# Forming the low halves of split weights by an accumulating DMA instead of a VectorE subtraction

## The chip, the core and the metric

The kernel runs on one core of one Trainium2 chip. The metric is the device time of one execution in microseconds (us): the median of several runs, and beside it one execution taken by the hardware profiler, from which every row below comes. The engines are called as in the profile: PE is TensorE's matmul side and PEld its weight loads, DVE is VectorE, ACT is ScalarE, POOL is GpSimd, and SP is the engine that here only issues transfers. Sixteen DMA engines move the data between memory and the core.

## The reference, cut to what matters

Two decoder layers work on 272 tokens (16 meta tokens and 256 of the input) of width 1024. All matrix products are taken in float32:

```
for l in range(2):
    h = rms_norm(x, norm1_g[l])
    u = h @ w_in[l]                       # 1024 x 6560, split among three mixers and their gates
    y_a = conv_module(...); y_b = mla(...); y_c = hgrn2(...)
    mix = gate_a * y_a + gate_b * y_b + gate_c * y_c
    x = x + mix @ w_out[l]                # 1024 x 1024
    h2 = rms_norm(x, norm2_g[l])
    x = x + square(relu(h2 @ w_ff1[l])) @ w_ff2[l]   # 1024 x 4096 x 1024
return x[:, 16:]
```

The weights are read once: 146 MB in all, most of it w_in, w_ff1 and w_ff2.

## The kernel before, in words

A float32 product is made of three matmuls in the reduced type float32r. Every weight and every activation is split into a high part, which is the value rounded to float32r, and a low part, which is the value minus its high part. The helper `mm3` then adds high by high, low by high and high by low (lines 208, 209 and 210).

The weights come in pieces of 128 partitions by 1024 columns of float32, 512 KB each. There are 276 such pieces, and each serves 24 matmuls. `piece` (line 193) brings one: `fetch` (line 104) has SP load it into a buffer `wraw`, of which there are three; ACT rounds it into `whi` (line 198), of which there are four; DVE subtracts `whi` from `wraw` into `wlo` (line 200), of which there are four as well. A `wraw` buffer is free for the next load when ACT and DVE have both read it. A `whi` or `wlo` buffer is free when PE has used the last of its columns.

Each layer has two parts. In the mixer part (66 pieces: w_in, the two latent projections and the branches' output projections) the tiles of `h @ w_in` alternate with the steps of the attention, the HGRN2 recurrence and the convolution, whose small operations lie on DVE, ACT, POOL and PE; the order is set by rates in the code. In the feed-forward part (72 pieces: w_out, w_ff1, w_ff2) there is little besides the pieces and their matmuls.

The order on each engine comes from the framework's scheduler. `piece` raises its priority by `AHEAD` = 500, so that loads and splits are put well ahead of their use; after that each engine and each queue works strictly in its order. POOL has only small work: memsets, copies and the powers that make the norms' factors (`rsqrt`, line 213; lines 352, 703, 754, 806). It issues no transfer.

Of the kernel before, what the change touches and what calls it, by code (L numbers as in the profile page):

```python
# [44 lines left out]

# Column tiles of w_in, in the order in which they are computed.
N_HEAD_TILES = 28
# [17 lines left out]

# Columns of the block of per-partition parameters (per layer).
PP = {}
# [7 lines left out]

# Columns of the block of constants.
CC = {}
# [9 lines left out]
def block_kernel(ctx, tc, xT_d, pp_d, cc_d, win_d, wuq_d, wukv_d, wbr_d, wout_d, wff1_d, wff2_d, out_d):  # L87
# [14 lines left out]

    # ---------------------------------------------------------------- inputs and constants
    def fetch(src, n=1024):
# [71 lines left out]

    # ---------------------------------------------------------------- helpers
    def psum_acc():
# [14 lines left out]
    def piece(src, raw=None):  # L193
        """1024 columns of weights, as their high and low parts in float32r."""
        with tc.high_priority(offset=AHEAD):
            raw = raw or fetch(src)
            hi = wsp.tile([P, 1024], F32R, name="whi", tag="whi", bufs=4)
            act.copy(out=hi, in_=raw)  # L198
            lo = wsp.tile([P, 1024], F32R, name="wlo", tag="wlo", bufs=4)
            dve.tensor_tensor(out=lo, in0=raw, in1=hi.bitcast(F32), op=SUB)  # L200
        return hi, lo
# [13 lines left out]
    def spread_rows(r, dst, wins, t0):  # L215
        """dst[:, t - t0] = r of token t on every partition; r holds a column for each window of tokens."""
        n = len(wins)
        dg = small.tile([P, 3, P], F32, name="dg", tag="dg", bufs=1)
        dve.tensor_tensor(
            out=dg[:, :n, :], in0=ident.unsqueeze(1).broadcast_to([P, n, P]),  # L220
            in1=r.unsqueeze(2).broadcast_to([P, n, P]), op=MUL)
        for j, (w, a, b) in enumerate(wins):
            pe.matmul(dst[:, a - t0:b - t0], ones, dg[:, j, a - w:b - w], start=True, stop=True)
# [3 lines left out]
    def rms_spread(sq, wcol, wins, t0, rtile=None):  # L227
        """1 / sqrt(eps + the sum over the partitions of sq * wcol) for each token, on every partition."""
        sm = psum_sm()
        n = len(wins)  # L230
        for j, (w, _, _) in enumerate(wins):
            pe.matmul(sm[:, j:j + 1], sq[:, w:w + P], wcol, start=True, stop=True)
        me = small.tile([P, 4], F32, name="me", tag="me")
        dve.tensor_scalar(out=me[:, :n], in0=sm[:, :n], scalar1=EPS, scalar2=None, op0=ADD)
        r = rtile if rtile is not None else small.tile([P, 4], F32, name="r", tag="r")
        rsqrt(r[:, :n], me[:, :n], n)
        b = psum_mx()
        spread_rows(r[:, :n], b, wins, t0)
        return b
# [4 lines left out]
    def add_square(dst, x, k):  # L244
        """dst becomes, or gains, x * x."""
        if k == 0:
            act.activation(out=dst, in_=x, func=AF.Square)
        else:
            n = x.shape[1]
            q = small.tile([P, L], F32, name="sqx", tag="sqx", bufs=1)  # L250
            act.activation(out=q[:, :n], in_=x, func=AF.Square)
            dve.tensor_tensor(out=dst, in0=dst, in1=q[:, :n], op=ADD)
# [4 lines left out]
    def scale_input(xg, l, k):  # L257
        """x * g, before the first norm's division."""
        ins = act.activation(out=xg[0][:, k, :], in_=xT[:, k, :], func=AF.Copy, scale=par(l, "n1g", k))
        dve.scalar_tensor_tensor(out=xg[1][:, k, :], in0=xT[:, k, :], scalar=par(l, "n1g", k),  # L260
                                 in1=xg[0][:, k, :].bitcast(F32), op0=MUL, op1=SUB)
        return ins

    # ---------------------------------------------------------------- lower bounds of the second layer
    lb = const.tile([P, 8, HH], F32, name="lb")
# [12 lines left out]

    # ---------------------------------------------------------------- layers
    for l in range(DEPTH):  # L280
# [4 lines left out]

        # h = RMSNorm(x) * g
        if l == 0:
# [49 lines left out]

        # ------------------------------------------------------------ u = h @ w_in
        tiles = win_tiles()
# [19 lines left out]
        def rope_keys(j):  # L359
            """The shared rotary keys: 32 columns, as four sums of two of the eight terms, on 32 partitions each."""  # L360
            with tc.high_priority(offset=AHEAD):
                raw = first["kr"] if l == 0 else fetch(win_d[l, j], KD * ROPE)
                by_term = raw[:, :KD * ROPE].rearrange("p (k j) -> p k j", k=KD)
                dve.tensor_tensor(out=wkr, in0=by_term, in1=par(l, "n1g", 0, KD).unsqueeze(2).broadcast_to([P, KD, ROPE]), op=MUL)
            ps = psum_hx()
            for k in range(KD):
                b = k % 4 * ROPE
                pe.matmul(ps[b:b + ROPE, :L], wkr[:, k, :], xT[:, k, :], start=(k < 4), stop=(k >= 4))
            act.copy(out=krT, in_=ps[:, :L])
# [48 lines left out]

        # ------------------------------------------------------------ latent projections
        def latent_steps():  # L420
# [108 lines left out]

        # ------------------------------------------------------------ attention  # L530
        def attention_steps():
# [7 lines left out]
            def finish(w, po):  # L539
                """The heads' outputs for the queries of a tile, with the channels on the partitions."""  # L540
                r = rows(w)
# [36 lines left out]
            def scores(w, c):  # L578
                """Of a pair of heads: exp(q k - max) / its sum."""
                nk, mx, hs = WIN[w] + P, maxs[w], slice(2 * c, 2 * c + 2)  # L580
# [27 lines left out]
            def turned(w, pr):  # L608
                """The weights of a head, with the keys on the partitions."""
                pt = psum_pt()[:, :3 * P].rearrange("p (w t) -> p w t", w=3)  # L610
# [27 lines left out]

        # ------------------------------------------------------------ HGRN2
        def hgrn_steps():  # L640
# [15 lines left out]

            # weights of the keys s in a tile for the queries t of the same tile
            at = {w: by_head(half(f"at{w}", "h", 8)) for w in (1, 2)}
# [10 lines left out]
            for hp in range(2):  # L669
# [3 lines left out]

                # blocks of 8 tokens
                dd, ep, en = pair("dd"), pair("ep"), pair("en")
# [20 lines left out]

                # the later half of a block of 16, 32 or 64 tokens against its earlier half
                for hs in (8, 16, 32):
# [30 lines left out]

                # chunks of 64 tokens against earlier chunks  # L730
                q1, k1 = pair("q1"), pair("k1")
# [37 lines left out]

            # v, with the tokens on the partitions  # L770
            yield after("i", HH - 1)
# [8 lines left out]

            # outputs of the heads, their norm (the queries still lack the first norm's factor) and gate
            rp = small.tile([P, 4], F32, name="rp", tag="rp", bufs=1)
# [35 lines left out]

        # ------------------------------------------------------------ convolution
        def conv_steps():  # L820
# [11 lines left out]
            def channel_mean(src):  # L832
                """Rows that add up to the mean over the channels."""
                part = psum_mx()
# [29 lines left out]

        # ------------------------------------------------------------ merge of the branches, under their gates
        gates = {}
        mix = {}

        def gate_tile(i):
            """tanh(u / 2) of a gate u; its sigmoid is (1 + tanh(u / 2)) / 2."""  # L870
            ps = win_acc(N_HEAD_TILES + i, T0)
# [27 lines left out]

        # ------------------------------------------------------------ the order of the parts  # L900
        dense = [(head_tile, j) for j in range(NLAT, N_HEAD_TILES)] + [(gate_tile, i) for i in range(NGATE)]
# [26 lines left out]

        # ------------------------------------------------------------ x += mix @ w_out, and the second norm
        ffn = tc.tile_pool(name=f"ffn{l}", bufs=1)  # L930
# [22 lines left out]

        # ------------------------------------------------------------ feed-forward
        fhi = fp.tile([P, KF, L], F32R, name="fhi")
# [33 lines left out]

# [1 line left out]
def _constants():  # L991
# [31 lines left out]
def _pack(w, kt, cols):  # L1023
    """(..., K, M) -> (..., M / cols, 128, kt * cols), with row k * 128 + p of the columns on partition p."""
    lead = w.shape[:-2]
# [72 lines left out]
```

## Time and profile before

| | |
|---|---|
| median of 3 runs | 965.31 us (964.18 to 965.49) |
| profiled execution, span from first to last instruction | 965.4 us |
| busy PE, PEld | 954.1 us, 906.3 us |
| busy DVE, ACT, POOL | 709.2 us, 521.3 us, 47.0 us |
| mean granted TensorE clock | 0.996 of 2.4 GHz |
| bytes moved | 149.18 MB, 155 GB/s over the span |

The span and the median agree within 0.1 us, so sums are made against the span. Busy times are sums over instructions of one engine; matmuls are pipelined, so a PE that shows as busy is not PE at its peak.

### The profile page before, as it was taken

The page shows a single profiled execution, that of the slowest core. Times are in us where ns is not written, and L with a number is a line of the kernel's source. Part 1 is how long each engine was busy: PE and PEld are TensorE (multiplying, and loading weights), DVE is VectorE, ACT ScalarE, POOL GpSimd, SP SyncE. Part 2 cuts the span into 40 slices and gives each one's busy share as a digit, 9 for nine tenths or more (in the row PEclk, how much of TensorE's full clock was granted, in tenths as well). Part 3 has the DMA queues.
Part 4 walks back from the last instruction along what each step waited for, and adds up shares of the span by engine and source line. Part 5 has one row for each costly group of instructions (what it writes and reads, how often), then busy time and mean ns, then how long its engine had stood idle before and what let it go on. Part 6 is the DMA issues. An engine that isn't in the chain of part 4 may idle for free.

```text
span 965.4 us, 18801 instructions
## 1 busy us (share of the span) xinstructions
PE 954.1 (99%) x7578; PEld 906.3 (94%) x7578; DVE 709.2 (73%) x1315; ACT 521.3 (54%) x941; POOL 47.0 (5%) x73
## 2 busy tenths in 40 slices
PE   7999999999999999999999999999999999999998
PEld 6989988888999999999999899888899999999998
DVE  6888998874887866655557899989759887765552
ACT  6575765543536655544436576665445566563331
POOL 2103100000000000000000021000000000000000
PEclk9999999998999999999999999999999999999999
DMA  8444333332455555555554444333334565556561
GB/s 276 149 141 153 110 111 109 110 114 84 154 173 176 175 174 176 175 175 174 175 180 153 131 154 152 107 114 111 131 122 164 161 202 192 188 184 194 192 202 60
DMA packets 42423, 149.18 MB, mean 155 GB/s; under 512 B 4704, under 2 KB 6368, under 8 KB 42336
## 3 DMA queue, kind: packets, MB, share of 16 engines
q1 hardware_dynamic: 40608, 146.10, 46.8%
q10 hardware_dynamic: 1728, 1.88, 0.6%
q8 instruction: 59, 0.97, 0.4%
q14 instruction: 28, 0.23, 0.1%
HBM read 146.91 MB, written 1.05 MB: 153 GB/s over the span
## 4 chain that ended last, share of the span: by engine, by line
PE 96%; DVE 2%; DMA 2%; ACT 1%; issue 0%; ACTq 0%
PE acc L208 18%; PE acc L210 18%; PE acc L209 18%; PE hx L208 9%; PE hx L210 9%; PE hx L209 9%; PE sm L633 2%; PE mx L588 1%; PE pt L612 1%; PE hx L714 1%; DVE wlo L200 1%; PE sm L473 1%; PE hx L797 1%; DMA wraw<-in_win_dram 1%; PE mx L836 1%; PE hx L796 1%
## 5 line engine op out<-in xcount | busy, mean ns | idle before, releaser
L200 DVE TENSOR_TENSOR wlo<-wraw,whi 128x1024 fp32r<-128x1024 f32 x276 | 337.6, 1224 | 183.8 <-ACT whi L198 183.0
L198 ACT CAST whi<-wraw 128x1024 fp32r<-128x1024 f32 x276 | 289.2, 1049 | 338.6 <-PE acc L210 187.6
L208 PE MATMUL acc<-hhi,whi 128*128 128x272 f32 (+1 forms) x704 | 208.0, 296 | 0.0
L209 PE MATMUL acc<-hhi,wlo 128*128 128x272 f32 (+1 forms) x704 | 204.3, 290 | 0.0
L210 PE MATMUL acc<-hlo,whi 128*128 128x272 f32 (+1 forms) x704 | 203.7, 290 | 0.0
L208 PEld LDWEIGHTS acc<-hhi,whi 128*128 128x128 f32 x704 | 133.7, 190 | 7.9 <-issue 4.8
L210 PEld LDWEIGHTS acc<-hlo,whi 128*128 128x128 f32 x704 | 133.5, 190 | 3.1 <-issue 1.7
L209 PEld LDWEIGHTS acc<-hhi,wlo 128*128 128x128 f32 x704 | 133.9, 190 | 1.6 <-issue 0.6
L829 DVE SCALAR_TENSOR_TENSOR cacc<-hpad,pph,cacc 128x272 f32<-128x272 f32 (+1 forms) x240 | 110.3, 486 | 0.3
L210 PE MATMUL acc<-xlo,whi 128*128 128x272 f32 (+1 forms) x256 | 73.1, 286 | 0.0
L208 PE MATMUL acc<-xhi,whi 128*128 128x272 f32 (+1 forms) x256 | 73.1, 286 | 0.0
L210 PE MATMUL hx<-xlo,whi 128*128 128x272 f32 (+1 forms) x256 | 73.0, 285 | 0.0
L209 PE MATMUL hx<-fhi,wlo 128*128 128x272 f32 (+1 forms) x256 | 72.9, 285 | 0.0
L208 PE MATMUL hx<-xhi,whi 128*128 128x272 f32 (+1 forms) x256 | 72.9, 285 | 0.0
L209 PE MATMUL acc<-xhi,wlo 128*128 128x272 f32 (+1 forms) x256 | 72.9, 285 | 0.0
L209 PE MATMUL hx<-xhi,wlo 128*128 128x272 f32 (+1 forms) x256 | 72.9, 285 | 0.0
L209 PE MATMUL acc<-fhi,wlo 128*128 128x272 f32 (+1 forms) x256 | 72.9, 285 | 0.0
L208 PE MATMUL acc<-fhi,whi 128*128 128x272 f32 (+1 forms) x256 | 72.8, 284 | 0.0
L208 PE MATMUL hx<-fhi,whi 128*128 128x272 f32 (+1 forms) x256 | 72.8, 284 | 0.0
L210 PE MATMUL hx<-flo,whi 128*128 128x272 f32 (+1 forms) x256 | 72.7, 284 | 0.0
L210 PE MATMUL acc<-flo,whi 128*128 128x272 f32 (+1 forms) x256 | 72.7, 284 | 0.0
L208 PEld LDWEIGHTS acc<-xhi,whi 128*128 128x128 f32 x256 | 48.3, 189 | 0.1
(344 smaller groups left out, 2115.6 us busy)
## 6 DMA issues: line engine op xcount, KB each, us to landing
wraw<-in_wff_dram SPq DMA_DIRECT2D x128, 512.0 KB, 4.2
wraw<-in_win_dram SPq DMA_DIRECT2D x102, 512.0 KB, 3.4
wraw<-in_wbr_dram SPq DMA_DIRECT2D x24, 512.0 KB, 3.3
wraw<-in_wout_dram SPq DMA_DIRECT2D x16, 512.0 KB, 3.4
wraw<-in_wuq_dram SPq DMA_DIRECT2D x4, 512.0 KB, 3.8
xT<-in_xT_dram SPq DMA_DIRECT2D x4, 272.0 KB, 5.1
wraw<-in_wukv_dram SPq DMA_DIRECT2D x2, 512.0 KB, 3.8
out_dram<-xT ACTq DMA_DIRECT2D x8, 128.0 KB, 3.6
```

The source lines that it names most:

```text
L198: act.copy(out=hi, in_=raw)
L200: dve.tensor_tensor(out=lo, in0=raw, in1=hi.bitcast(F32), op=SUB)
L208: pe.matmul(out, whi, xhi, start=start, stop=False)
L209: pe.matmul(out, wlo, xhi, start=False, stop=False)
L210: pe.matmul(out, whi, xlo, start=False, stop=stop)
L473: pe.matmul(sums[32 * h:32 * h + 32, :L], sel96[:QK, g, :], msq_[:QK, h, :], start=(g == 0), stop=(g == 1))
L588: pe.matmul(sh, qT[h // 4][:, h % 4, WIN[w]:WIN[w] + P], kT[h // 4][:, h % 4, :nk], start=True, stop=False)
L612: pe.transpose(pt[:WROWS[kw], 2 - kw, :], pr[:, WIN[kw]:WIN[kw] + WROWS[kw]], ident)
L633: pe.matmul(place(po, h, P), vv[kw][:WROWS[kw], h * VD:(h + 1) * VD], pts[h % 2][:WROWS[kw], 2 - kw, :], start=(kw == 0), stop=(kw == w))
L714: pe.matmul(ps[:, w - 1, h, :], kl[:, h, WIN[w]:WIN[w] + P], ql[:, h, q0:q0 + 64], start=True, stop=True)
L796: pe.matmul(o, at[w][:, h, :], vtok[w][:, hc], start=True, stop=False)
L829: dve.scalar_tensor_tensor(out=a, in0=hpad[:, c, T0 + k:T0 + k + N], scalar=hpar(l, "cw", c * CK + k), in1=a, op0=MUL, op1=ADD)
```

## The change

The subtraction on DVE is taken out. In its place ACT writes the negated high part into `wlo`, and POOL then issues a transfer that reads the same raw weights from memory a second time and adds them onto what `wlo` holds. The rest of the diff takes out comments and docstrings and keeps the line numbers up to here.

```diff
             hi = wsp.tile([P, 1024], F32R, name="whi", tag="whi", bufs=4)
             act.copy(out=hi, in_=raw)
             lo = wsp.tile([P, 1024], F32R, name="wlo", tag="wlo", bufs=4)
-            dve.tensor_tensor(out=lo, in0=raw, in1=hi.bitcast(F32), op=SUB)
+            act.activation(out=lo, in_=hi.bitcast(F32), func=AF.Copy, scale=-1.0)
+            nc.gpsimd.dma_start(out=lo, in_=src, accum_op=ADD)
         return hi, lo
```

## Rows read from the trace of the kernel before

**Rows 1.** The page: the engines' busy times, and the chain that ended last.

```profile
PE 954.1 (99%) x7578; PEld 906.3 (94%) x7578; DVE 709.2 (73%) x1315; ACT 521.3 (54%) x941; POOL 47.0 (5%) x73
...
PE 96%; DVE 2%; DMA 2%; ACT 1%; issue 0%; ACTq 0%
PE acc L208 18%; PE acc L210 18%; PE acc L209 18%; PE hx L208 9%; PE hx L210 9%; PE hx L209 9%; PE sm L633 2%; PE mx L588 1%; PE pt L612 1%; PE hx L714 1%; DVE wlo L200 1%; PE sm L473 1%; PE hx L797 1%; DMA wraw<-in_win_dram 1%; PE mx L836 1%; PE hx L796 1%
```

**Rows 2.** The page's costliest groups: busy us, mean ns of one; idle time before, releaser.

```profile
L200 DVE TENSOR_TENSOR wlo<-wraw,whi 128x1024 fp32r<-128x1024 f32 x276 | 337.6, 1224 | 183.8 <-ACT whi L198 183.0
L198 ACT CAST whi<-wraw 128x1024 fp32r<-128x1024 f32 x276 | 289.2, 1049 | 338.6 <-PE acc L210 187.6
```

**Rows 3.** Windows: the four parts (mixer 1, feed-forward 1, mixer 2, feed-forward 2).

```profile
core 0: us, PE busy (x) PEld busy (x) DVE busy (x) ACT busy (x) POOL busy (x), PEclk, DMA share, GB/s
0.00:276.70 276.70, 270.17 (x2052) 243.56 (x2053) 223.46 (x475) 157.85 (x317) 27.39 (x53) 0.99 0.43 139
276.70:500.60 223.90, 223.90 (x1783) 223.67 (x1782) 144.18 (x210) 113.64 (x174) 0.00 (x0) 1.00 0.54 175
500.60:757.80 257.20, 256.27 (x2033) 235.61 (x2033) 214.92 (x453) 148.97 (x299) 19.57 (x20) 1.00 0.42 136
757.80:963.50 205.70, 203.75 (x1718) 203.49 (x1716) 126.67 (x179) 100.84 (x151) 0.00 (x0) 1.00 0.56 176
```

**Rows 4.** ACT in order of time, feed-forward 2: start, duration, idle before.

```profile
822.01 1.05 ACT L198 CAST whi<-wraw 128x1024 fp32r<-128x1024 f32 x1 [1.06 <-PE acc L210]
822.97 0.37 ACT L966 ACTIVATE rl<-acc 128x256 f32<-128x256 f32 x1
823.37 0.42 ACT L967 ACTIVATE fhi<-rl 128x256 fp32r<-128x256 f32 x1
824.85 1.05 ACT L198 CAST whi<-wraw 128x1024 fp32r<-128x1024 f32 x1 [1.06 <-PE hx L210]
```

**Rows 5.** DMA, whole run: the queues, and the share of 16 engines' span.

```profile
q1 hardware_dynamic: 40608, 146.10, 46.8%
q10 hardware_dynamic: 1728, 1.88, 0.6%
```

**Rows 6.** DMA from 5 to 10 us alone: packets, rate, the one queue's share.

```profile
DMA packets 746, 1.99 MB, mean 398 GB/s; under 512 B 80, under 2 KB 80, under 8 KB 746
...
q1 hardware_dynamic: 746, 1.99, 102.6%
```

**Rows 7.** The tile wraw: issues of its loads, and their time to landing.

```profile
L106 SPq DMA_DIRECT2D wraw<-in_wff_dram x128: 327/328/775, 294.4 to 944.0; - x128
...
DMA to landing us min/median/max: 2.2/3.4/6.5
```

**Rows 8.** What POOL waited for: us in total, times, longest.

```profile
POOL qq L352 <- ACT whi L198: 257.6, 1, 257.6
POOL ss L806 <- DVE ss L805: 102.2, 5, 29.4
POOL kl L703 <- DVE kl L709: 67.5, 8, 14.0
POOL kl L703 <- ACT en L679: 64.0, 3, 25.9
```

**Rows 9.** POOL's own instructions by line: busy us, mean ns.

```profile
L213 POOL TENSOR_TENSOR rq<-rq,mhalf 128x24 f32<-128x24 f32 (+1 forms) x2 | 8.0, 3986 | 9.7 <-DVE rq L485 9.7
```

**Rows 10.** DVE in order of time, at the start: the first low part.

```profile
7.82 1.23 DVE L200 TENSOR_TENSOR wlo<-wraw,whi 128x1024 fp32r<-128x1024 f32 x1
```

## The prediction, made before the changed kernel was run

> **What bounds the kernel now.** The first view is the page's list of busy times beside the chain that ended last. PE is busy for 954.1 us of a span of 965.4 us, and 96% of the chain is PE; the reader is to see that DVE, though 73% busy, holds only 2% of the chain, of which the subtraction of line 200 is about half [rows 1]. The second view is the windows of the four parts. I cut them where the first matmul of each part starts: 276.7, 223.9, 257.2 and 205.7 us, together 963.5 us, with 1.9 us around them. In both feed-forward parts PE has no idle time worth naming, while DVE, ACT and the DMA engines (share 0.54 and 0.56) are between half and two thirds used; in the mixer parts DVE is busy 81 to 84% and the DMA share is 0.42 to 0.43 [rows 3]. A piece of weights (24 matmuls) thus takes PE 223.9 / 72 = 3.11 us and 205.7 / 72 = 2.86 us in the feed-forward parts, and a mixer part has one piece every 276.7 / 66 = 4.19 or 257.2 / 66 = 3.90 us. The third view is ACT in order of time: it copies a high part when PE releases the buffer, one each 2.84 us, so the split runs at PE's pace, three pieces ahead of it [rows 4].
>
> So there is next to nothing to win by a faster split, and the question is whether the new way of making a low part still delivers one every 2.86 to 4.19 us.
>
> **What is taken away.** 276 subtractions of 1.224 us, 337.6 us of DVE [rows 2]. They lie beside matmuls; on the chain they are about 1% of the span, up to 9.7 us [rows 1]. The raw buffer comes free earlier, since DVE no longer reads it. I count no gain, because what replaces them is longer on the same path.
>
> **What is added on ACT.** 276 negations of 128x1024. The trace has none; the nearest row is the cast of the same size on the same engine, 1.049 us [rows 2]. That makes 66 x 1.05 = 69 us more in a mixer part and 72 x 1.05 = 76 us more in a feed-forward part. ACT then has 158 + 69 = 227 of 276.7, 149 + 69 = 218 of 257.2, 114 + 76 = 190 of 223.9 and 101 + 76 = 177 of 205.7 us [rows 3]. It fits under PE everywhere; cost nothing, and the cover shrinks to 14% in the last part.
>
> **What is added on POOL.** 276 issues. No transfer of POOL's is in the trace. Below, SP's issue takes 0.33 us [rows 7]; above, POOL's dearest instruction takes 3.99 us [rows 9]. Even 4 us would stay under the price that I put on a piece below (4.41 us), so I count none and leave the queue's order for the rivals.
>
> **What is added on the DMA engines.** This is the term that decides. The 276 pieces are read a second time, which by itself doubles the traffic, and the second reading must also fetch what the low part holds, add, and write back. A plain load is priced by two rows. Over the run, 46.8% of 965.4 us for 146.10 MB is 451.8 us, so a piece of 0.524 MB costs 1.62 us of all 16 engines [rows 5]. Between 5 and 10 us, with the engines full (share 102.6%), the rate is 398 GB/s, so a piece costs 1.32 us [rows 6].
>
> An add has no row. Below, it costs what a load does (1.32 to 1.62 us): the second operand's fetch hidden entirely behind the first's. Above, it runs alone and takes the longest time that a load took from issue to landing, 6.5 us [rows 7]. I take two loads, 2.6 to 3.2 us: a packet that adds has two operands of 4 KB to fetch and one to write, and a load is priced by fetching one; nothing in these rows suggests that an engine fetches two in the time of one.
>
> Nothing in the rows shows an adding transfer, so the doubling is my reading of the bytes. The Trainium skill, "Collectives: The Full Stack", section "The bandwidth ceiling: the fold count and why AG ≠ RS ≠ AR", says that a reducing transfer is slower than a copying one not for the addition but for its two source reads, with measured rates of 62.28 against 32.35 GB/s. By that rule an add costs 1.93 loads, which as an estimate from that page gives 276 x 1.62 x 2.93 = 1310 us at the dearer price of a load; no run here shows it yet.
>
> **The sum.** A piece costs load + add = three loads: 3.95 us at the full rate and 4.86 us at the mean rate. Each part lasts as long as the slower of PE and the DMA engines. At 3.95 us the mixer parts need 261 us (PE's 276.7 holds in the first, 261 in the second) and each feed-forward part 284: 277 + 284 + 261 + 284 = 1106 us. At 4.86 us they need 321 and 350: 1342 us. After the change there will be one or two loads and one or two adds in flight, less than in the full stretch at the start and more than in the mean, so I take the middle, 4.41 us: 291 + 317 + 291 + 317 = 1216 us. The engines will not be full all the time: a low part's buffer goes round from PE's release over cast (1.05), negation (1.05), issue, landing (3.4 us in the median for a load, some 6 for an add) and PE's use (about 3 us), some 12 us, and four buffers give one piece per 3 us: below 4.41, but near enough for gaps. I put these at 5%, 61 us, a choice. The first low part, done at 9.05 us now [rows 10], comes some 4 us later. 1216 + 61 + 4 gives 1280 us with the rest around it. Against the median: span and median agree within 0.1 us.
>
> **The rivals.**
>
> *The add is no dearer than a load, and hidden.* Then a piece costs 2.63 to 3.24 us. It is not slower as long as this is under feed-forward 2's 2.86 us, that is, as long as an add costs under about 1.24 to 1.54 us. For it: the share of 0.56 leaves room for one more load at the full rate [rows 3, 6]. Against it: the second operand. At 2.63 us the parts stay as they are, 965 us, or down to 956 if the 1% of the chain on line 200 goes without replacement; at 3.24 us the feed-forward parts take 233 each, 10 + 28 us more, 1003 us. Chance 0.16, of which 0.07 not slower.
>
> *The add costs three loads or more,* since operands arrive one after the other and packets wait inside an engine. Then a piece costs 5.27 to 6.48 us: 1454 to 1789 us for 276; at the 6.5 us bound with a load of 1.62 beside it, 276 x 8.1 = 2241 us. For it: the landing of 3.4 us in the median is already twice the 1.62 us of transfer [rows 5, 7], so serial steps cost. Chance 0.27.
>
> *POOL's order stalls PE.* POOL works in order, and an add behind a power or a memset that waits for DVE waits too; PE then lacks its low part. The waits are long: 29.4, 25.9 and 14.0 us [rows 8]. Three pieces ahead are about 12 us of cover in a mixer part, most of which cast, negation and landing already use. The three largest groups after the first (the memset of line 352, which only waits for the layer) sum to 234 us; if all counted on top, and the transfers were hidden, 965 + 234 = 1199 us. But POOL waits long now because it has nothing else to do, and the scheduler will place the adds before such waits. The mark would be PE idle in the mixer parts, not in the feed-forward parts. Chance 0.07.
>
> TensorE's clock is not a rival of its own: it was granted 0.99 in mixer 1 and 1.00 elsewhere [rows 3]. If it fell to its lower level, 1.2 GHz, in PE's new gaps, a piece would take up to 2 x 2.86 = 5.7 us, within the second rival's times.
>
> **How the numbers follow.** The forecast (an add of about two loads, 1106 to about 1400 us) has 0.50, the rivals 0.16, 0.27 and 0.07. The time is that of the forecast, 1280 us. Its own range is 1106 to 1400. The range for 8 in 10 leaves out the cheaper half of the hidden case below, and above the part of the dear case beyond its 1789 us: 1000 to 1800 us. A measurement of this kernel cannot tell less than about 0.2% (1.9 us) from no change. Faster by more than that needs the hidden case and the chain's 1% won: 0.04. Within it: 0.03. Slower: 0.93.
>
> **What would show it.** In the changed profile DVE's busy time should fall by about 338 us, ACT's rise by about 290, the bytes moved rise from 149 to about 290 MB or more, and the DMA share stand near 0.95 in the feed-forward parts. PE should show idle time before line 209 (the matmul by the low part) that a POOL transfer into wlo ends, and the feed-forward parts should grow by more (in per cent) than the mixer parts. The chain should pass from PE to DMA. If instead PE's gaps lie in the mixer parts alone, POOL's order was the cause; if the DMA share stays below 0.8 while PE waits, latency or POOL's issue time, and not the engines' throughput, was the limit, and my sum would be right or wrong by accident. The step that can fail worst is the price of one add.

## The result and the profile after

The changed kernel takes 1180.05 us (1177.35 to 1180.76) against 965.31 us: 1.2217 times as long, 95% interval 1.2196 to 1.2238. That is slower, as forecast, and within the range; the forecast of 1280 us was 100 us too high.

The page of the changed kernel, to be read beside [rows 1] and [rows 5] (matmul lines stand one line lower than before; q0 is POOL's new queue, q1 SP's):

```profile
PE 1018.3 (86%) x7578; PEld 931.9 (79%) x7578; DVE 408.1 (35%) x1039; ACT 777.4 (66%) x1217; POOL 281.7 (24%) x349
...
q0 software_dynamic: 39744, 144.72, 64.9%
q1 hardware_dynamic: 40608, 146.10, 33.1%
...
DMA 52%; PE 39%; issue 5%; ACT 3%; POOL 1%; DVE 0%; SPq 0%; POOLq 0%; ACTq 0%
DMA wlo<-in_wff_dram 33%; DMA wlo<-in_win_dram 11%; PE acc L210 9%; PE acc L211 8%; PE acc L209 8%; DMA wlo<-in_wbr_dram 4%; DMA wlo<-in_wout_dram 4%; PE hx L210 3%; PE hx L211 2%; PE hx L209 2%; PE sm L634 2%; PE pt L613 1%; PE mx L589 1%; PE hx L715 1%; ACT wlo L200 1%
```

The chain that was 96% PE is now 52% DMA, all of it transfers into `wlo`. The two queues hold the answer on the price: 64.9% of 1178.6 us for 276 adds is 2.77 us an add, and 33.1% for 146.10 MB is 1.40 us a load of one piece. By these prices an add costs 1.98 loads, and a piece 4.17 us of all 16 engines.

For the parts I cut each run at the same events: the first matmul on the merged mix (L208/L209 with mhi) in each layer, and the first rotary-key matmul of layer 2. Windows of the changed kernel:

```profile
0.00:303.50 303.50, 275.50 (x2052) 246.25 (x2053) 154.75 (x410) 219.18 (x385) 82.63 (x120) 0.99 0.96 238
303.50:581.80 278.30, 236.16 (x1713) 222.06 (x1711) 58.74 (x134) 176.74 (x242) 61.80 (x72) 0.98 1.04 269
581.80:892.00 310.20, 277.27 (x2041) 249.50 (x2041) 142.90 (x376) 210.08 (x363) 76.01 (x88) 0.95 0.94 229
892.00:1178.60 286.60, 229.37 (x1781) 214.11 (x1779) 51.66 (x122) 171.43 (x228) 61.26 (x71) 1.00 1.02 264
```

By the same cut, the last two parts of the kernel before are a little different from those in [rows 3], which I had cut 7 us later:

```profile
500.60:750.40 249.80, 248.87 (x1971) 228.21 (x1971) 207.71 (x437) 145.62 (x293) 19.57 (x20) 1.00 0.41 136
750.40:965.40 215.00, 211.15 (x1781) 210.89 (x1779) 133.88 (x195) 104.19 (x157) 0.00 (x0) 1.00 0.55 174
```

The cut between feed-forward 1 and mixer 2 does not divide the work alike in the two kernels, as the counts of PE's matmuls show: 1713 and 2041 after, 1783 and 1971 before. In the changed kernel the last three pieces of feed-forward 1, but for one matmul, come behind the first rotary-key matmul. Here is one of their three lines of `mm3` in mixer 2's window, with the first and last start in us behind the durations in ns; the other two have 24 matmuls each as well:

```profile
L209 PE MATMUL hx<-fhi,whi x24: 284/287/292, 581.6 to 592.8; 128*128 128x272 f32 x24
```

The work of feed-forward 1 ends at 593.3 us, 11.5 us behind the cut. With these 11.5 us counted to feed-forward 1, the parts grew by 27, 66, 49 and 72 us, 213 in all: 29% and 33% in the feed-forward parts, 10% and 20% in the mixer parts. The 72 adds of feed-forward 1 were all issued by 581.0 us, so for the DMA engines the window up to the cut is the right one.

The last three columns are clock, DMA share and GB/s: the share is 1.02 to 1.04 in the feed-forward parts. GB/s counts what arrives, so for an add one of its two operands. If an add is counted with both, feed-forward 1 fetches 72 x 3 x 0.524 MB in 278.3 us, 407 GB/s, and feed-forward 2 395 GB/s. That is the full rate of 398 GB/s in [rows 6]. The two queues in feed-forward 1 alone:

```profile
q0 software_dynamic: 10300, 37.49, 68.5%
q1 hardware_dynamic: 10326, 37.20, 35.4%
```

Neither queue fills the engines' time, and both together do (104%). So it is the engines that are full and not POOL's queue, as far as these shares tell; the adds on two queues were not tried.

What PEld waited for, over the whole run (it and PE show one gap twice), and the landing of the adds, from the tile wlo:

```profile
PEld acc L210 <- DMA wlo<-in_wff_dram: 57.1, 63, 3.6
PEld hx L210 <- DMA wlo<-in_wff_dram: 51.2, 57, 1.6
PEld acc L210 <- DMA wlo<-in_win_dram: 39.3, 23, 5.7
```

```profile
L201 POOL DMA_DIRECT2D wlo<-in_wff_dram x128: 862/862/881, 338.4 to 1165.1; - x128
...
DMA to landing us min/median/max: 5.2/9.3/12.2
```

PE stops at line 210, the matmul by the low part, for about a microsecond at nearly every piece of the feed-forward parts (63 + 57 waits for the 128 pieces of w_ff1 and w_ff2). An add lands 9.3 us after its issue in the median, where a load of before landed after 3.4 [rows 7]; beside the adds a load now lands after 8.0.

### The profile page after: what moved, and what is told of

It is laid out like the page before. It is cut to its first block, busy times and chain, and to the rows that moved or that the text cites. A ratio compares the mean times of both kernels' runs of the same rounds, so it can differ in the third digit from the quotient of the medians.

```text
span 1178.6 us, 19348 instructions
## 1 busy us (share of the span) xinstructions
PE 1018.3 (86%) x7578; PEld 931.9 (79%) x7578; DVE 408.1 (35%) x1039; ACT 777.4 (66%) x1217; POOL 281.7 (24%) x349
## 3 DMA queue, kind: packets, MB, share of 16 engines
q0 software_dynamic: 39744, 144.72, 64.9%
q1 hardware_dynamic: 40608, 146.10, 33.1%
HBM read 291.62 MB, written 1.05 MB: 248 GB/s over the span
## 4 chain that ended last, share of the span: by engine, by line
DMA 52%; PE 39%; issue 5%; ACT 3%; POOL 1%; DVE 0%; SPq 0%; POOLq 0%; ACTq 0%
DMA wlo<-in_wff_dram 33%; DMA wlo<-in_win_dram 11%; PE acc L210 9%; PE acc L211 8%; PE acc L209 8%; DMA wlo<-in_wbr_dram 4%; DMA wlo<-in_wout_dram 4%; PE hx L210 3%; PE hx L211 2%; PE hx L209 2%; PE sm L634 2%; PE pt L613 1%; PE mx L589 1%; PE hx L715 1%; ACT wlo L200 1%
## 5 line engine op out<-in xcount | busy, mean ns | idle before, releaser
L200 ACT ACTIVATE wlo<-whi 128x1024 fp32r<-128x1024 f32 x276 | 290.5, 1054 | 4.1 <-ACT whi L198 2.2
L210 PE MATMUL acc<-hhi,wlo 128*128 128x272 f32 (+1 forms) x704 | 210.8, 299 | 29.6 <-DMA wlo<-in_win_dram 29.6
L209 PE MATMUL acc<-hhi,whi 128*128 128x272 f32 (+1 forms) x704 | 212.6, 302 | 2.4 <-ACT scrahi L391 2.4
L211 PE MATMUL acc<-hlo,whi 128*128 128x272 f32 (+1 forms) x704 | 208.6, 296 | 0.0
L201 POOL DMA_DIRECT2D wlo<-in_wff_dram x128 | 110.5, 863 | 386.3 <-ACT wlo L200 314.6
L210 PEld LDWEIGHTS acc<-hhi,wlo 128*128 128x128 f32 x704 | 138.6, 197 | 35.5 <-DMA wlo<-in_win_dram 33.9
L201 POOL DMA_DIRECT2D wlo<-in_win_dram x102 | 89.2, 878 | 298.8 <-ACT wlo L200 193.7
L209 PEld LDWEIGHTS acc<-hhi,whi 128*128 128x128 f32 x704 | 138.3, 196 | 6.6 <-ACT scrahi L391 2.6
L211 PEld LDWEIGHTS acc<-hlo,whi 128*128 128x128 f32 x704 | 138.5, 197 | 0.9 <-issue 0.3
L210 PE MATMUL hx<-fhi,wlo 128*128 128x272 f32 (+1 forms) x256 | 75.9, 296 | 18.7 <-DMA wlo<-in_wff_dram 18.7
L969 DVE TENSOR_TENSOR rl<-rl 128x272 f32<-128x272 f32 (+1 forms) x64 | 27.7, 433 | 180.7 <-ACT fhi L968 180.7
L209 PE MATMUL acc<-xhi,whi 128*128 128x272 f32 (+1 forms) x256 | 73.5, 287 | 0.0
L209 PE MATMUL hx<-xhi,whi 128*128 128x272 f32 (+1 forms) x256 | 72.8, 285 | 0.0
```

The source lines that it names most:

```text
L200: act.activation(out=lo, in_=hi.bitcast(F32), func=AF.Copy, scale=-1.0)
L201: nc.gpsimd.dma_start(out=lo, in_=src, accum_op=ADD)
L209: pe.matmul(out, whi, xhi, start=start, stop=False)
L210: pe.matmul(out, wlo, xhi, start=False, stop=False)
L211: pe.matmul(out, whi, xlo, start=False, stop=stop)
L969: dve.tensor_tensor(out=rl[:, :N], in0=rl[:, :N], in1=rl[:, :N], op=MUL)
```

## The experiments

Theory A: an add costs the DMA engines about two loads because it fetches two operands, and their throughput sets the pace of the feed-forward parts. Against it stand B (a transfer of POOL's in the path costs by its issue, latency and order), C (the negation on ACT costs), D (the second read of the weights from memory costs) and E (the way round the four buffers is too long). The table gives the time, its ratio to the kernel before with the 95% interval, and the four parts (M mixer, F feed-forward) of the profiled execution in us. The last column, late, says how long after the cut between F1 and M2 the last matmul of feed-forward 1 ends. Where a run that has late matmuls is compared with one that has none, they belong to F1 and not to M2. The cuts between M and F can be off too, by up to one piece (some 20 matmuls, 3 to 4 us): in e2, e3, e5 and e10.

| kernel | time | ratio | M1 | F1 | M2 | F2 | late |
|---|---|---|---|---|---|---|---|
| before | 965.3 | | 277 | 224 | 250 | 215 | 0.1 |
| changed | 1180.1 | 1.2196 to 1.2238 | 304 | 278 | 310 | 287 | 11.5 |
| e1 plain second load | 1034.1 | 1.0694 to 1.0735 | 293 | 227 | 280 | 232 | 10.5 |
| e2 add from wraw | 1398.7 | 1.4463 to 1.4541 | 348 | 347 | 340 | 369 | 10.0 |
| e3 negation alone | 991.0 | 1.0255 to 1.0289 | 279 | 230 | 260 | 220 | 0.1 |
| e4 every second piece | 1044.3 | 1.0806 to 1.0855 | 292 | 244 | 268 | 244 | 0.1 |
| e5 three buffers | 1385.6 | 1.4325 to 1.4381 | 361 | 322 | 355 | 344 | 16.2 |
| e6 mixer pieces only | 1048.2 | 1.0840 to 1.0880 | 311 | 225 | 295 | 215 | 0.1 |
| e7 feed-forward pieces only | 1110.9 | 1.1490 to 1.1529 | 274 | 279 | 265 | 291 | 12.0 |
| e8 negation on DVE | 1149.2 | 1.1873 to 1.1938 | 300 | 272 | 289 | 286 | 11.1 |
| e9 seven gate buffers | 1194.5 | 1.2321 to 1.2424 | 323 | 277 | 305 | 286 | 11.2 |
| e10 five buffers | 1168.8 | 1.2088 to 1.2127 | 306 | 276 | 295 | 289 | 11.5 |
| e11 add from wraw, five of them | 1184.7 | 1.2255 to 1.2296 | 310 | 284 | 297 | 292 | 9.3 |
| e12 every third mixer piece | 982.7 | 1.0158 to 1.0216 | 283 | 224 | 258 | 215 | 0.0 |

**A plain second load.**

```diff
-            nc.gpsimd.dma_start(out=lo, in_=src, accum_op=ADD)
+            nc.gpsimd.dma_start(out=lo, in_=src)
```

> The second transfer of each piece stays on POOL's queue, with its wait on the negation and its landing before the matmul, but is a plain load instead of an add, so that the low part holds the raw weights (the products are not the reference's). Theory A (an add costs the 16 DMA engines about two loads, and their throughput sets the pace): a piece falls from one load and one add (1.41 + 2.77 us by the changed kernel's queues) to two loads, 2.6 to 2.9 us, under PE's 2.86 to 4.19 us: 965 to 1010 us. Theory B (a POOL transfer in the path is the cost, by its issue of 0.86 us, its landing and its place in a strict order): the time stays above 1100 us. Theory C (the negation on ACT is the cost): it stays near 1180 us.

It took 1034.1 us. Of the 213 us, 147 go when the transfer no longer adds, 106 of them in the feed-forward parts. The queues of this run and its F1 up to the cut:

```profile
q0 software_dynamic: 39744, 144.72, 44.8%
q1 hardware_dynamic: 40608, 146.10, 40.8%
```

```profile
293.00:520.40 227.40, 219.04 (x1710) 216.77 (x1708) 58.53 (x133) 176.78 (x242) 37.83 (x72) 0.99 0.97 329
```

POOL's order and the wait on the negation are out as the main cause, since they are still there. The issue became shorter, 0.53 us against 0.86, and the landing too, 5.3 us in the median against 9.3, so B's latency is left to the runs with other numbers of buffers. The time is 24 us over my upper figure. The 66 us that stay over before are spread over all four parts, with the late matmuls counted to F1: 16, 14, 19 and 17 us. In the mixer parts the DMA share is about 0.8, so there, over the whole part, something other than throughput costs.

Two things limit what this run tells. The share is 0.97 in F1 at only 329 GB/s, against 398 in [rows 6]: a share near 1 does not by itself show that the engines move all they can. And a plain load on POOL's queue costs 44.8% of 1031.6 us for 276, 1.67 us; against that an add costs 1.66 loads and not 1.98. So "two loads" is a round figure.

**The add's operand from the core instead of memory.**

```diff
-            nc.gpsimd.dma_start(out=lo, in_=src, accum_op=ADD)
+            nc.gpsimd.dma_start(out=lo, in_=raw, accum_op=ADD)
```

> The add takes its raw operand from the buffer wraw, already on the core, instead of reading the weights from memory again; the result is the same. Theory A (two operands fetched by the same DMA engine): an add costs much the same 2.5 to 2.8 us, and the time stays between 1130 and 1200 us; a little more is possible because wraw is now held until the add has landed, with three such buffers. Rival D (the second read of 145 MB from memory is the cost, that is, bandwidth of memory): the time falls to 965 to 1010 us.

A miss: 1398.7 us, far over my figure. SP's own waits show why, and that this run does not tell A from D:

```profile
SPq L106 <- DMA wlo<-wraw: 1262.9, 273, 10.3
```

Every load waited for an add to release one of three `wraw` buffers. The later run with five of them answers the question.

**The negation alone**, put ahead of the old subtraction.

```diff
             lo = wsp.tile([P, 1024], F32R, name="wlo", tag="wlo", bufs=4)
+            act.activation(out=lo, in_=hi.bitcast(F32), func=AF.Copy, scale=-1.0)
             dve.tensor_tensor(out=lo, in0=raw, in1=hi.bitcast(F32), op=SUB)
```

> The kernel before, with ACT's negation of the high part into wlo put ahead of the subtraction, which then overwrites it: the ACT work of the change alone, and a wait of DVE for it. Theory A: hidden under PE, 964 to 972 us. Theory C (ACT's extra 290 us are a cost of their own): over 1000 us.

It took 991.0 us, 25.7 more than before: neither nothing nor the 1000 us of C. ACT is busy 776.9 us here, 79%. PE's waits for the low part make only 7.0 us of it (three waits, the longest 3.2):

```profile
PE acc L210 <- DVE wlo L201: 7.0, 3, 3.2
```

PE is also busy 9.6 us longer, at a mean clock of 0.989 against 0.996, and waits a little more for other results of ACT and DVE. Which of these the longer work on ACT brings about, and how, is not shown.

**Every second piece.** A count in `piece` chooses between the two ways.

```diff
+            if count[0] % 2 == 0:
+                (negation and add)
+            else:
+                (subtraction on DVE)
```

> Every second piece is made by negation and add, the others by DVE's subtraction. Theory A: the DMA engines need 1.41 + 2.77 / 2 = 2.8 us for a piece in the mean, under PE's 2.86 to 4.19 us, so 965 to 1000 us, far below half of the added 215 us. Theory B or C (each add or negation has a price of its own in the path): about half of the added time, 1050 to 1090 us.

It took 1044.3 us, 37% of the added time, between A's figure and that of B or C, so this run does not decide between them. A's price was too low: the queues (40.3% of 1047.1 us for 276 loads, 40.5% for 138 adds) give 1.53 us a load and 3.07 an add here, 3.07 us a piece in the mean, over PE's 2.86 in F2 and just under its 3.11 in F1. The parts lasted 244 / 72 = 3.39 us a piece at a share of 0.93 and 0.89; why they lasted longer than either was not tried.

**Three buffers instead of four.**

```diff
-            hi = wsp.tile([P, 1024], F32R, name="whi", tag="whi", bufs=4)
+            hi = wsp.tile([P, 1024], F32R, name="whi", tag="whi", bufs=3)
```

(`wlo` likewise.)

> The changed kernel with three whi and three wlo buffers instead of four. Theory A (throughput of the DMA engines) in the feed-forward parts: with fewer transfers in flight each lands sooner, and the parts stay within 10% of 278 and 287 us; the shortest way round, 2.1 us of cast and negation, 0.9 of issue, 5.2 of the shortest landing and 3 of PE, is 11.2 us for three, 3.7 us a piece. Rival E (the way round the buffers is the limit, with the landing of 9.3 us as it is): 15.3 us for three buffers, 5.1 us a piece, 367 us a feed-forward part, above 1400 us in all. In the mixer parts, where I suspect the way round, both give more: 330 to 380 us each.

F1 and F2 grew by 16% and 20%, between the two theories; the adds landed in 7.4 us in the median. One buffer fewer costs time, so with three the way round counts. The sum (2.1 + 0.9 + 7.4 + 3) / 3 = 4.5 us a piece is F1's 322 / 72, but that shows nothing by itself: with four buffers (2.1 + 0.9 + 9.3 + 3) / 4 = 3.8 us is as near to F1's 278 / 72 = 3.9, since a landing that grows in a full queue is part of the way round. Whether the way round is the limit with four needed the opposite edit.

**One kind of part at a time**: the same choice by `(count[0] - 1) % 138 < 66`, and its opposite.

> Negation and add for the 132 pieces of the mixer parts, DVE's subtraction for the 144 of the feed-forward parts. If the parts are independent: the mixer parts as in the changed kernel (about 304 and 310 us against 277 and 250), the feed-forward parts as before (224 and 215): 1050 us. If the transfers run across the border (a backlog carried from part to part), the mixer parts come out shorter than 300.

> The other half: negation and add for the 144 pieces of the feed-forward parts, subtraction in the mixer parts. Theory A: 72 pieces at one load and one add (three operands of 0.52 MB at about 400 GB/s, 3.9 us) make 278 and 287 us; mixer parts as before, 277 and 250: about 1090 us. If the cost is POOL's order among its other work, which lies in the mixer parts alone, the feed-forward parts stay near 224 and 215 and the time under 1000 us.

They took 82.5 and 145.1 us more than before, together 228 against the change's 215: the two kinds of part are nearly independent. (E7's M2 of 265 us holds 12.0 us of late matmuls; without them it is 253, against 250 before.) E7's feed-forward parts (279 and 291) are those of the changed kernel, although POOL's own work lies in the mixer parts; POOL's order is not the cause there.

**The negation on DVE**, from `wraw`, beside the cast.

```diff
-            act.activation(out=lo, in_=hi.bitcast(F32), func=AF.Copy, scale=-1.0)
+            dve.tensor_scalar(out=lo, in0=raw, scalar1=-1.0, scalar2=None, op0=MUL)
```

> The changed kernel with the negation taken from ACT to DVE, straight from wraw (its rounding to float32r gives the negated high part), so that it runs beside the cast and no longer behind it; the adds stay. Theory A: the feed-forward parts stay at 278 and 287 us, since the DMA engines set them. If ACT's extra work and the longer way to the add cost the mixer parts their time, those fall from 304 and 310 towards 290, and the whole to 1145 to 1165 us; if POOL's or the transfers' latency costs it, the whole stays within 1170 to 1185 us.

It took 1149.2 us, 31 less than the changed kernel. The way to the add is over a microsecond shorter, DVE needs 0.70 us where ACT needed 1.05, yet F1 and F2 gain only 6 and 0.5 us: the landing grew from 9.3 to 10.2 us. M1 and M2 gain 4 and 21. This is the best version with every low part added, and still 19% slower than before.

**Seven gate buffers**, for room (`NGATE = 7`), as the control; then five `whi` and `wlo` buffers; then the add from `wraw` with five `wraw` buffers.

> A control for the next two: the changed kernel with 7 gate buffers instead of 15, which frees 8.5 KB a partition and makes the merge of the branches begin earlier in the order of the mixer parts. The feed-forward parts should stay at 278 and 287 us; the mixer parts may come out longer, and are not compared with those of the changed kernel.

> The control with five whi and five wlo buffers. Theory A (throughput): the DMA engines are full in the feed-forward parts with four already, so the parts stay at 270 to 287 us and the landing grows instead, from 9.6 to about 13 us. Rival E (the way round the buffers, landing unchanged): 15.6 us for five, 3.1 us a piece, 225 to 230 us a part.

> The control with the add's raw operand taken from wraw, as in the earlier run, but with five wraw buffers, so that the next loads need not wait for the adds. Theory A (two operands through the same engines, wherever they come from): feed-forward parts of 265 to 295 us. Rival D (the second read from memory costs): 225 to 235 us.

The control's feed-forward parts are those of the changed kernel. With a fifth buffer they stay (276 and 289), and the landing takes up most of the longer way round, 12.5 us against 9.4:

```profile
305.80:581.50 275.70, 236.42 (x1732) 220.49 (x1730) 59.54 (x136) 186.81 (x243) 61.69 (x72) 1.00 1.05 274
```

```profile
DMA to landing us min/median/max: 5.0/12.5/15.0
```

E is out for four buffers in the feed-forward parts. In the mixer parts the fifth buffer takes 17 and 11 us off the control's (a piece of each, 3 to 4 us, is only the cut's), so there the way round does count. With the add from `wraw`, the second read from memory is gone and the feed-forward parts stay at 284 and 292:

```profile
q0 software_dynamic: 39744, 144.72, 64.1%
q1 hardware_dynamic: 40608, 146.10, 33.5%
...
HBM read 146.91 MB, written 1.05 MB: 125 GB/s over the span
```

64.1% of 1182.7 us is 2.75 us an add, close to the 2.77 of the changed kernel. D is out as the main cause: with e1, it is the adding that costs, not where the raw operand comes from.

**Every third piece of the mixer parts**, with the negation on DVE.

> The only place where the DMA engines had room: every third piece of the mixer parts by negation (on DVE, 0.7 us) and add, all other pieces by subtraction. DVE loses 44 x 0.5 us. If DVE's load holds up the mixer parts anywhere, 955 to 963 us; since PE sets the pace, I expect no gain: 963 to 985 us, the adds' landing of 6 to 8 us costing a little where pieces come close together.

It took 982.7 us, 1.8% more than before. The share in M1 is only 0.64, so the DMA engines had room, and still 44 adds cost 17 us; by which step of their way was not tried. No version tried beats the kernel before.

## Why the prediction was right, and where it was off

**What is taken away** gave nothing, as said. DVE fell by 301 us, not 338: its busy time is a union, and neighbouring instructions overlap by about 0.1 us.

**The DMA engines** were the term that decides, and an add costs about two loads: 1.98 by the queues, 1.93 in e11 with the raw operand on the core, 1.66 against the plain load of e1. The Trainium skill, "Collectives: The Full Stack", section "The bandwidth ceiling: the fold count and why AG ≠ RS ≠ AR", has the two source reads of the add halve the rate of ReduceScatter against AllGather among four ranks, a measured ratio of 1.93; the trace agrees with it at 1.98 and 1.93, for another kind of transfer. That the second fetch is the reason, and not the addition, no run here shows.

**The choice of the rate** was the mis-sized term. I took the middle, 4.41 us a piece, between the full rate's 3.95 and the mean rate's 4.86. The DMA engines served the feed-forward parts at 278.3 / 72 = 3.87 and 286.6 / 72 = 3.98 us a piece: the full rate. Kept full by two queues, they ran here at the price of [rows 6], not of [rows 5]. That put F1 (290 us with its late matmuls) and F2 27 and 30 us too high.

**The gaps** of 61 us, on top, were wrong for the feed-forward parts, where the engines have none; the five buffers show it. These two terms are 118 us too much; the mixer parts, 303.5 and 298.7 (without the late matmuls) where the sum had 291 each, gave 20 back, which leaves 98 of the 101 us between 1280 and the profiled 1178.6.

**The mixer parts** were rightly said to grow less (10% and 20% against 29% and 33%), but for a reason of which I had half. Their mean demand, a piece per 3.90 to 4.19 us, hides that pieces come close together in some stretches. Here is layer 2's mixer in two windows of 20 us:

```profile
720.00:740.00 20.00, 20.00 (x153) 17.07 (x152) 17.97 (x47) 16.55 (x38) 4.87 (x6) 1.00 1.04 257
840.00:860.00 20.00, 16.44 (x122) 15.69 (x121) 2.77 (x6) 9.66 (x13) 3.65 (x5) 0.83 0.71 171
```

In the one the engines are full and PE is fed; in the other PE has gaps at a share of 0.71, which throughput does not explain. E8 and e10 show that a shorter way to the add and one more buffer both take time off these parts, and e1 that a plain second load leaves 16 and 19 us there. How the remainder divides between latency, ACT's order and the order that the scheduler chose is open.

**The negation at nothing** is a step that failed: "it fits under PE everywhere" counted ACT's busy time, not what its longer work holds up. Alone it costs 25.7 us (e3), and with it on DVE instead of ACT the changed kernel gains 31 (e8). How much of this is the longer way from PE's release to the low part, and how much other work that ACT delays, stays open: in e3 the waits for the low part were 7.0 us.

**POOL** was right: 0.86 us an issue, within the bounds of 0.33 and 3.99, and its long waits shrank (the 29.4 us of [rows 8] to 3.3) now that adds stand in between. **The start** was under-counted: the first matmul by a low part of line 210 comes at 18.7 us, where the same matmul stood at 9.8 us before: 9 us later, not 4.

Of the rivals, the hidden add is refuted by e1 against the changed kernel, the dear add by the queues, and POOL's order, for the feed-forward parts, by e7.

## What to carry to other kernels

An accumulating transfer takes work from a compute engine and gives the DMA engines two loads' worth of it; count three loads a tile against the DMA engines' full rate, before looking at the engine that is relieved. Relieving an engine off the chain won nothing here, and what replaced it also lengthened the way from a buffer's release to its next use. To tell full DMA engines from a long way round, add a buffer: if the landing grows and the time stays, the engines are full. A sum of the way round divided by the number of buffers cannot tell the two apart, since the landing in it already holds the waiting. And when parts of two kernels are compared, count the matmuls in each part: the order on an engine can shift work across a cut.

## What the runs showed that was not expected

The DMA engines' share reads over 1 when they are full (1.02 to 1.06), and the rate of fetched operands, with an add counted as two, hardly depends on where they lie: 395 to 407 GB/s in the changed kernel's feed-forward parts, and by the same count 387 to 399 where the add took its raw operand from the core (e11). The Trainium skill, "DMA: Bandwidth & Descriptors", section "Specifications", has 435 GB/s as the ceiling of the fabric to the core's memory; the rates counted here stay under it.

TensorE's granted clock fell where PE had gaps: 0.76 of 2.4 GHz on the mean, a mix of its two levels, where PE had been busy for 16.14 of the 20 us before.

```profile
660.00:680.00 20.00, 16.14 (x108) 13.89 (x106) 11.70 (x27) 19.94 (x33) 8.55 (x8) 0.98 0.76 191
680.00:700.00 20.00, 16.59 (x116) 16.20 (x117) 8.68 (x25) 11.09 (x21) 7.38 (x8) 0.76 0.89 207
```

In the feed-forward parts, with a gap at nearly every piece, it stayed at 0.98 and 1.00. Whether and by how much the slower stretch adds to M2 was not tried.
